# A Mamba mixer's input norm: where the second chunk's squares are taken, when its factors are requested, and how the third chunk's squares are added

## The chip, the cores and the metric

The program runs on one core of a Trainium2 chip. TensorE (PE) multiplies matrices, VectorE (DVE), ScalarE (ACT) and GpSimd (POOL) work on elements, and SyncE (SP) issues the transfers. Each engine works through its own list of instructions in order and waits on semaphores for the others. The metric is the device time of one execution in microseconds (us). TensorE's clock has two levels, 1.2 and 2.4 GHz; the profile gives the granted share of the higher one (0.50 or 1.00).

## The reference

One inference step of a two-layer decoder trunk: a Mamba-2 mixer with its MLP, then sliding-window attention with its MLP. The change is in the first operation of the mixer, the norm of its input, and touches the projection that follows:

```python
def rmsnorm(x, w):
    xf = x.astype(jnp.float32)
    xf = xf * lax.rsqrt(jnp.mean(xf * xf, axis=-1, keepdims=True) + EPS)
    return (xf * w.astype(jnp.float32)).astype(x.dtype)

def mamba_mixer(h, conv_state, ssm_state, norm_w, w_in, ...):
    zxbcdt = rmsnorm(h, norm_w) @ w_in
    ...
```

The model width is 1024. There are 1104 columns (tokens): 1024 of the prompt, 64 of the sample and 16 learned ones.

## The kernel before

Activations lie with the model width on the partitions: eight tiles of 128 rows (k = 0 to 7), and the 1104 columns in three chunks. The program's list of chunks (`CH`) holds (0, 384), (384, 384) and (768, 336); the mixer works on them in the order 2, 0, 1. This document calls them the first chunk (index 2, 336 columns), the second (index 0) and the third (index 1, 384 columns each). The lists of instructions of the engines are made by a scheduler that orders the whole program by its own estimate of times, so the order in the code is a wish and not a rule.

For each chunk the input norm goes through these steps:

1. `load_h` (L318) loads the input tiles `xt` in four pairs of k.
2. `sums_x` squares the eight tiles (L329, on ACT, into `xsq`), and sums over the partitions with a product of each square with a constant matrix `ones_r` (L333, on PE, plain fp32). With `add=True` the two squares of a pair are first added on DVE (L331), which halves the number of these sum products from eight to four. The buffers of `xsq` come from a ring of five (L237).
3. `rstd_x` makes the factors n = 1/sqrt(mean + eps) as exp(-0.5 ln(.)) on ACT: a Ln (L340) and an Exp (L342), each with a load of its function table ahead of it.
4. `norm_x` multiplies each tile by the norm's weight and the factors on DVE (L353), rounds it to the high part with a cast on ACT (L354), and takes the difference, the low part, into `S` (L356): on DVE for even k, on POOL for odd k.
5. `conv_mms` multiplies the chunk by the weights of two units, B and C: for each k three products per unit, high by high (L568), high weight by low part (L569), low weight by high part (L570); 48 products a chunk. The next steps copy the results out of PSUM on ACT (L579 to L583).

The weights of these two units are split in the same stretch: a cast on ACT (L170) and a difference of 128x1024 on POOL (L171) for each. After the third chunk's products follow those of the step sizes (L435, L436) and of the next units.

In the kernel before, the first chunk's squares are added in pairs; those of the second and third are not, and all are taken on ACT. The factors of the second and third chunk are asked for in one call, after the first chunk's products.

Of the kernel before, what the change touches and what calls it, by code (L numbers as in the profile page):

```python
# [10 lines left out]
AF = mybir.ActivationFunctionType  # L11
ALU = mybir.AluOpType
# [129 lines left out]
class Kernel:  # L142
# [175 lines left out]
            self.nc.sync.dma_start(out=hp[kp], in_=self.i["x"][:, 2 * kp:2 * kp + 2, o:o + n])  # L318
        return hp

    def sums_x(self, c, hp, tag, add=False):

        nc = self.nc
        n = CH[c][1]
        ms = self.psa.tile([P, 512], F32, tag=tag, bufs={"y": 2}.get(tag, 1), name="xms")
        for kp, h in enumerate(hp):
            sq = [self.n1("xsq")[:, :n] for _ in range(2)]
            for j in range(2):
                nc.scalar.activation(out=sq[j], in_=h[:, j], func=AF.Square)  # L329
            if add:  # L330
                nc.vector.tensor_tensor(out=sq[0], in0=sq[0], in1=sq[1], op=ALU.add)  # L331
            for j in range(1 if add else 2):
                nc.tensor.matmul(out=ms[:, :n], lhsT=self.ones_d, rhs=sq[j], start=(kp + j == 0),  # L333
                                 stop=(kp == 3 and (add or j == 1)))
        return ms[:, :n]
# [1569 lines left out]
    def mixer(self, c1):  # L1905

        nc = self.nc
        mp = self.pool("mixc", ctx=c1)
        self.sp = self.pool("sp", ctx=c1)
        self.psa = self.pool("psa", bufs=1, space=PSUM, ctx=c1)  # L1910
        xs, fm = {}, {}
        hp = {2: self.load_h(2)}
        us = [self.conv_unit(0, nm) for nm in ("B", "C")]
        hp[0] = self.load_h(0)
        hp[1] = self.load_h(1)
        self.mixer_consts(mp)
        ms2 = self.sums_x(2, hp[2], "cb", True)
        rs2 = self.rstd_x([ms2])[0]
        xs[2] = self.norm_x(2, hp[2], rs2)
        ms0 = self.sums_x(0, hp[0], "st")  # L1920
        ms1 = self.sums_x(1, hp[1], "y")
        self.conv_mms(us, 2, xs)
        rs0, rs1 = self.rstd_x([ms0, ms1])
        for c, rs in ((0, rs0), (1, rs1)):
            xs[c] = self.norm_x(c, hp[c], rs)
            self.conv_mms(us, c, xs)
        draw = self.dt_product(mp, xs)
        ux = self.conv_unit(0, "x0")
        fm["B"], fm["C"] = (self.conv_rest(u) for u in us)
        for c in CORD:  # L1930
            self.conv_mm(ux, c, xs)
        fm["x0"] = self.conv_rest(ux)
        sums = self.dt_path(mp, draw)
        next(sums)
        ux = self.conv_unit(0, "x1")
        for k, c in enumerate(CORD):
            if k == 1:
                next(sums, None)
            self.conv_mm(ux, c, xs)
        next(sums, None)  # L1940
        fm["x1"] = self.conv_rest(ux)
        for g in range(G):
            gate = None
            if g + 1 == G:
                y = [self.fm([P, T], "gy") for j in range(2)]
                space = lambda c: ((self.sp.tile([P, 1024], F32, tag="bm", bufs=1, name="gt") if c == 1 else
                                    self.cw.tile([P, T], F32, tag="th", bufs=1, name="gt"))[:, :768]
                                   .rearrange("p (j n) -> p j n", j=2))
                gate = self.gate_group(0, xs, y, space, lambda: self.fm([P, T], "gm"))
            for t in self.ssd(g, fm):  # L1950
                for k in range({8: 2, 2: 1, 3: 1, 6: 1, 7: 1}.get(t, 0) if gate is not None else 0):
                    next(gate)
            if g + 1 < G:
                fm = self.group_in(g + 1, xs)
        nc.sync.dma_start(out=self.o["conv"], in_=self.cvo)
        for _ in gate:
            pass
        return xs
# [68 lines left out]
```

## Time and profile before

| | |
|---|---|
| device time, median of 3 runs | 2925.34 us (2923.25 to 2930.92) |
| the profiled execution: its own time | 2923.57 us |
| the profiled execution: span of its instructions | 2921.9 us |
| busy in the span: PE, DVE, ACT, POOL | 96%, 65%, 48%, 47% |
| share of the chain that ended last: PE, DVE, ACT | 77%, 10%, 4% |
| the stretch that the change touches | 0 to about 56 us of the span |

The profiled execution lasts 1.67 us longer than its span, which is what lies around the instructions. It is 1.8 us shorter than the median. The busy shares are means over the whole program; the change lies in the first 2% of it, where PE still waits for the others.

### The profile page before, as it was taken

The numbers are of one execution on the slowest core, as the hardware profiler recorded it, in microseconds if no ns is written. First come the engines' busy times: TensorE is split into PE (matmuls) and PEld (weight loads), VectorE is DVE, ScalarE is ACT, GpSimd is POOL, SyncE is SP. The second block draws the span as 40 slices with busy tenths as digits, with TensorE's granted clock in tenths as the row PEclk, the third lists the DMA queues.
The fourth block names the chain that finished last, engine by engine and source line by source line (L and its number), as shares of the span: only waits on it lengthen the run. The fifth ranks groups of instructions, "written<-read, shape, count | busy, mean of one in ns | idle before, by whom it ended". The sixth has DMA issues, their size and how long they took to land.

```text
span 2921.9 us, 51729 instructions
## 1 busy us (share of the span) xinstructions
PE 2816.2 (96%) x19895; PEld 2711.0 (93%) x19895; DVE 1895.0 (65%) x2995; ACT 1413.9 (48%) x2742; POOL 1386.1 (47%) x1279
## 2 busy tenths in 40 slices
PE   8999999988989999999999999999999999999998
PEld 6999999978889999999999999988889999999998
DVE  6788777765657675455466765666678454356675
ACT  6555555544555264444343325655555444433333
POOL 5566666665546615444266573312112444345562
PEclk9999999999999999999999999999999999999998
DMA  3344544447655224444554422447453444533422
GB/s 137 91 128 124 125 128 123 123 123 258 218 206 171 80 85 149 136 156 139 224 212 171 161 89 94 160 153 261 164 187 133 150 140 150 206 138 124 151 96 73
DMA packets 219470, 433.43 MB, mean 148 GB/s; under 512 B 30728, under 2 KB 128392, under 8 KB 216648
## 3 DMA queue, kind: packets, MB, share of 16 engines
q1 hardware_dynamic: 219224, 430.14, 44.3%
q8 instruction: 156, 2.56, 0.4%
q14 instruction: 90, 0.74, 0.1%
HBM read 302.71 MB, written 128.32 MB: 148 GB/s over the span
## 4 chain that ended last, share of the span: by engine, by line
PE 77%; DVE 10%; ACT 4%; issue 3%; DMA 3%; POOL 3%; SPq 0%; DVEq 0%; ACTq 0%; POOLq 0%
PE g L204 10%; PE g L206 10%; PE g L205 10%; PE mc L204 4%; PE mc L206 3%; PE mc L205 3%; PE ma L204 3%; PE ma L205 3%; PE ma L206 3%; PE md L206 3%; PE md L205 3%; PE md L204 3%; PE mb L206 3%; PE mb L204 3%; PE mb L205 3%
## 5 line engine op out<-in xcount | busy, mean ns | idle before, releaser
L1048 POOL TENSOR_TENSOR w<-s,w 128x384 fp32r<-128x384 f32 (+1 forms) x272 | 370.4, 1368 | 386.9 <-ACT w L1047 354.4
L206 PE MATMUL g<-S,w 128*128 128x384 f32 (+2 forms) x1584 | 531.1, 336 | 3.9 <-POOL w L171 3.3
L204 PE MATMUL g<-S,w 128*128 128x384 f32 (+2 forms) x1584 | 533.4, 337 | 1.3 <-DVE qp L1462 0.6
L205 PE MATMUL g<-S,w 128*128 128x384 f32 (+2 forms) x1584 | 533.6, 337 | 0.0
L1048 POOL TENSOR_TENSOR w<-raw,w 128x384 fp32r<-128x384 f32 (+1 forms) x204 | 264.3, 1301 | 286.2 <-ACT w L1047 255.2
L171 POOL TENSOR_TENSOR w<-raw,w 128x1024 fp32r<-128x1024 f32 x96 | 247.1, 2574 | 253.3 <-ACT w L170 189.3
L206 PEld LDWEIGHTS g<-S,w 128*128 128x128 f32 x1584 | 301.9, 191 | 5.8 <-POOL w L171 3.6
L204 PEld LDWEIGHTS g<-S,w 128*128 128x128 f32 x1584 | 301.3, 190 | 4.7 <-issue 1.5
L205 PEld LDWEIGHTS g<-S,w 128*128 128x128 f32 x1584 | 301.7, 190 | 0.9 <-issue 0.3
L1047 ACT CAST w<-s 128x384 fp32r<-128x384 f32 (+1 forms) x272 | 149.8, 557 | 313.0 <-DVE s L1172 84.7
L204 PE MATMUL ma<-S,w 128*128 128x276 f32 (+1 forms) x808 | 235.2, 291 | 8.0 <-DVE us L1264 6.7
L206 PE MATMUL ma<-S,w 128*128 128x276 f32 (+1 forms) x808 | 234.7, 290 | 0.0
L205 PE MATMUL ma<-S,w 128*128 128x276 f32 (+1 forms) x808 | 234.3, 290 | 0.0
L1047 ACT CAST w<-raw 128x384 fp32r<-128x384 f32 (+1 forms) x204 | 111.8, 555 | 154.6 <-PE mc L206 45.2
L602 DVE SCALAR_TENSOR_TENSOR fm<-xp,cv,fm 128x1024 f32<-128x1024 f32 x96 | 162.8, 1698 | 33.1 <-ACT fm L583 32.5
L204 PEld LDWEIGHTS ma<-S,w 128*128 128x128 f32 x808 | 153.3, 190 | 9.3 <-ACT S L1229 2.7
L205 PE MATMUL g<-R,w 128*128 128x384 f32 (+2 forms) x480 | 158.6, 330 | 0.0
L204 PE MATMUL g<-R,w 128*128 128x384 f32 (+2 forms) x480 | 158.1, 329 | 0.0
L206 PE MATMUL g<-R,w 128*128 128x384 f32 (+2 forms) x480 | 158.1, 329 | 0.0
L205 PEld LDWEIGHTS ma<-S,w 128*128 128x128 f32 x808 | 153.5, 190 | 0.0
L206 PEld LDWEIGHTS ma<-S,w 128*128 128x128 f32 x808 | 153.2, 190 | 0.0
L170 ACT CAST w<-raw 128x1024 fp32r<-128x1024 f32 x96 | 100.5, 1047 | 105.8 <-DMA raw<-in_w_o_dram 19.9
(492 smaller groups left out, 8696.0 us busy)
## 6 DMA issues: line engine op xcount, KB each, us to landing
raw<-in_w_up_dram SPq DMA_DIRECT2D x64, 512.0 KB
raw<-in_w_in_dram SPq DMA_DIRECT2D x48, 512.0 KB
raw<-in_w_downs_dram SPq DMA_DIRECT2D x64, 384.0 KB
w<-ws_o SPq DMA_DIRECT2D x48, 512.0 KB
w<-ws_q SPq DMA_DIRECT2D x40, 512.0 KB
ab<-acs_d SPq DMA_DIRECT2D x64, 256.0 KB
S<-t_d SPq DMA_DIRECT2D x18, 828.0 KB
S<-t_e SPq DMA_DIRECT2D x18, 816.0 KB
```

The source lines that it names most:

```text
L170: nc.scalar.copy(out=wh, in_=raw)
L171: nc.gpsimd.tensor_tensor(out=wl, in0=raw, in1=wh.bitcast(F32), op=ALU.subtract)
L204: mm(out=out, lhsT=wh, rhs=xh, start=(first and k == 0), stop=False)
L205: mm(out=out, lhsT=wh, rhs=xl, start=False, stop=False)
L206: mm(out=out, lhsT=wl, rhs=xh, start=False, stop=(k == n - 1))
L602: nc.vector.scalar_tensor_tensor(out=acc[:, :SEQ], in0=xp[:, k:k + SEQ], scalar=cv[:, j, k:k + 1], in1=acc[:, :SEQ], op0=ALU.mult, op1=ALU ...
L1047: nc.scalar.copy(out=t[:, 0], in_=src)
L1048: nc.gpsimd.tensor_tensor(out=t[:, 1], in0=src, in1=t[:, 0].bitcast(F32), op=ALU.subtract)
```

## The change

`sums_x` gets a parameter `vector`: the squares of that many pairs are taken on DVE, as the product of a tile with itself, and the rest on ACT. The mixer calls it for the second chunk with `vector=3`, so six of the eight squares move to DVE. The third chunk's squares are now added in pairs. The factors of the second chunk are asked for right after the first chunk's norm and ahead of its products, those of the third after the second's norm, each in a call of its own.

```diff
-    def sums_x(self, c, hp, tag, add=False):
+    def sums_x(self, c, hp, tag, add=False, vector=0):
...
             for j in range(2):
-                nc.scalar.activation(out=sq[j], in_=h[:, j], func=AF.Square)
+                if kp < vector:
+                    nc.vector.tensor_tensor(out=sq[j], in0=h[:, j], in1=h[:, j], op=ALU.mult)
+                else:
+                    nc.scalar.activation(out=sq[j], in_=h[:, j], func=AF.Square)
...
-        rs2 = self.rstd_x([ms2])[0]
-        xs[2] = self.norm_x(2, hp[2], rs2)
-        ms0 = self.sums_x(0, hp[0], "st")
-        ms1 = self.sums_x(1, hp[1], "y")
-        self.conv_mms(us, 2, xs)
-        rs0, rs1 = self.rstd_x([ms0, ms1])
-        for c, rs in ((0, rs0), (1, rs1)):
-            xs[c] = self.norm_x(c, hp[c], rs)
+        rs = {2: self.rstd_x([ms2])[0]}
+
+        ms = self.sums_x(0, hp[0], "st", vector=3)
+        for c, nx in ((2, 0), (0, 1), (1, None)):
+            xs[c] = self.norm_x(c, hp[c], rs[c])
+            if nx is not None:
+                rs[nx] = self.rstd_x([ms])[0]
+            if nx == 0:
+                ms = self.sums_x(1, hp[1], "y", True)
             self.conv_mms(us, c, xs)
```

The line numbers of the changed kernel are four higher from the squares on (the ACT squares L329 become L333, the factors' Ln L340 becomes L344), and the new squares on DVE are L331.

The first place is DVE's list from the pair sums of the first chunk's squares to the first chunk's differences. `xsq` are squares, `xt` the input tiles, `n` the factors, `S` the low parts. Before:

```order
L331 TENSOR_TENSOR xsq<-xsq 128x336 x4
L426 MEMSET w 128x8x32
L353 SCALAR_TENSOR_TENSOR xt<-xt,nv,n_232 128x336 x8
L356 TENSOR_TENSOR S<-xt,S 128x336 x4
L456 TENSOR_SCALAR an<-an 128x32
```

And in the changed kernel:

```order
L335 TENSOR_TENSOR xsq<-xsq 128x336 x4
L331 TENSOR_TENSOR xsq<-xt 128x384 x2
L430 MEMSET w 128x8x32
L357 SCALAR_TENSOR_TENSOR xt<-xt,nv,n_232 128x336 x2
L331 TENSOR_TENSOR xsq<-xt 128x384 x2
L357 SCALAR_TENSOR_TENSOR xt<-xt,nv,n_232 128x336 x6
L331 TENSOR_TENSOR xsq<-xt 128x384 x2
L360 TENSOR_TENSOR S<-xt,S 128x336 x4
L335 TENSOR_TENSOR xsq<-xsq 128x384 x2
```

The six squares of the second chunk stand two ahead of the first chunk's scalings, two among them and two between them and the first chunk's differences.

The second place is ACT's list around the second chunk's factors, which are `n_365` before and `n_284` in the change. Before, from the last squares that stand ahead of them:

```order
L329 ACTIVATE xsq<-xt 128x384 x3
L411 ACTIVATE cv<-cv 128x32x5
L455 ACTIVATE an<-an 128x32
L427 CAST w<-raw 128x8x32
L429 CAST w<-raw 128x8x32
L329 ACTIVATE xsq<-xt 128x384
L340 ACT_TABLE_LOAD
L340 ACTIVATE n_365<-xms,eps 128x384
L329 ACTIVATE xsq<-xt 128x384
L342 ACT_TABLE_LOAD
L342 ACTIVATE n_365<-n_365 128x384
```

And in the changed kernel, where all these squares are of the third chunk:

```order
L333 ACTIVATE xsq<-xt 128x384 x3
L415 ACTIVATE cv<-cv 128x32x5
L333 ACTIVATE xsq<-xt 128x384
L459 ACTIVATE an<-an 128x32
L344 ACT_TABLE_LOAD
L344 ACTIVATE n_284<-xms,eps 128x384
L333 ACTIVATE xsq<-xt 128x384
L431 CAST w<-raw 128x8x32
L433 CAST w<-raw 128x8x32
L333 ACTIVATE xsq<-xt 128x384
L346 ACT_TABLE_LOAD
L346 ACTIVATE n_284<-n_284 128x384
```

The two casts of `w` and one more square now stand between the Ln and the Exp.

The third place is ACT's list around the third chunk's factors, `n_366` before and `n_392` in the change. Before, after the second chunk's casts:

```order
L354 CAST S<-xt 128x384 x7
L340 ACT_TABLE_LOAD
L340 ACTIVATE n_366<-xms,eps 128x384
L342 ACT_TABLE_LOAD
L342 ACTIVATE n_366<-n_366 128x384
L579 COPY xp<-g 128x256
```

And in the changed kernel:

```order
L358 CAST S<-xt 128x384 x8
L583 COPY xp<-g 128x256
L585 COPY xp<-g 128x10x8
L587 ACTIVATE fm<-g,cv 128x336
L583 COPY xp<-g 128x256
L585 COPY xp<-g 128x10x8
L587 ACTIVATE fm<-g,cv 128x336
L344 ACT_TABLE_LOAD
L344 ACTIVATE n_392<-xms,eps 128x384
L346 ACT_TABLE_LOAD
L346 ACTIVATE n_392<-n_392 128x384
```

The six copies of the first chunk's results (B and C, three each) now stand ahead of the third chunk's factors; before they stood behind.

## Rows read from the trace of the kernel before

**Rows 1.** Stretches 46.53 to 119 us: busy us (instructions) of each engine, granted clock, DMA
```profile
46.53:55.39 8.86, 8.86 (x48) 8.21 (x48) 3.86 (x7) 1.63 (x3) 2.37 (x3) 1.00 0.34 118
55.39:119.00 63.61, 63.61 (x408) 59.88 (x407) 48.03 (x61) 32.76 (x71) 28.80 (x32) 1.00 0.27 77
```

**Rows 2.** Waits of PE, 21 to 119 us: total, times, longest
```profile
PE g L569 <- DVE S L356: 1.7, 2, 1.1
PE g L569 <- DVE dx L477: 1.3, 1, 1.3
PE g L568 <- ACT fm L583: 0.6, 1, 0.6
```

**Rows 3.** Chain that ended last, 14 to 56 us: start, us, what
```profile
14.74 6.06 DVE xt L353 x8
...
21.28 0.42 PE g L569
...
23.39 0.66 PE xms L333 x2
24.07 0.52 ACT xsq L329
...
28.21 0.53 ACT n L342
28.77 6.62 DVE xt L353 x8
...
35.94 1.28 ACT L340
...
39.13 0.53 ACT n L342
...
46.53 0.45 PE g L569
```

**Rows 4.** Timeline of DVE, single instructions: start, us, what
```profile
14.74 0.77 DVE L353 SCALAR_TENSOR_TENSOR xt<-xt,nv,n 128x336 f32<-128x336 f32 x1 [5.01 <-ACT n L342]
16.40 0.55 DVE L353 SCALAR_TENSOR_TENSOR xt<-xt,nv,n 128x336 f32<-128x336 f32 x1
17.36 1.20 DVE L353 SCALAR_TENSOR_TENSOR xt<-xt,nv,n 128x336 f32<-128x336 f32 x1
```

**Rows 5.** Timeline of POOL, single instructions
```profile
10.49 2.35 POOL L171 TENSOR_TENSOR w<-raw,w 128x1024 fp32r<-128x1024 f32 x1 [5.16 <-ACT w L170]
12.81 2.34 POOL L171 TENSOR_TENSOR w<-raw,w 128x1024 fp32r<-128x1024 f32 x1
17.18 1.01 POOL L356 TENSOR_TENSOR S<-xt,S 128x336 fp32r<-128x336 f32 x1 [2.03 <-ACT S L354]
```

**Rows 6.** Timeline of SP's queue: an issue that waited for the second chunk's first pair
```profile
11.65 0.34 SPq L410 DMA_DIRECT2D cv<-in_cv_dram  x1
```

**Rows 7.** Timeline of PE's loads and products: two sums early, one late
```profile
13.36 0.34 PEld L333 LDWEIGHTS xms<-xsq,ones_r 128*128 128x128 f32 x1 [0.30 <-issue]
14.00 0.34 PEld L333 LDWEIGHTS xms<-xsq,ones_r 128*128 128x128 f32 x1 [0.30 <-issue]
...
29.86 0.81 PE L333 MATMUL xms<-xsq,ones_r 128*128 128x384 f32 x2
30.21 0.61 PE L570 MATMUL g<-S,w 128*128 128x336 f32 x1
```

**Rows 8.** Stretches around an idle time of PE at 2182 us, columns as in rows 1
```profile
2182.31:2185.75 3.44, 0.00 (x0) 0.03 (x1) 3.44 (x8) 0.00 (x0) 0.00 (x0) 1.00 1.06 396
2186.20:2189.60 3.40, 3.40 (x11) 2.99 (x10) 3.40 (x8) 0.00 (x0) 0.00 (x0) 0.50 1.05 415
```

**Rows 9.** Timeline of ACT: a weight cast, and the copies of the first chunk's results
```profile
22.84 0.39 ACT L427 CAST w<-raw 128x256 fp32r<-128x256 f32 x1
...
39.56 0.36 ACT L579 COPY xp<-g 128x256 f32<-128x256 f32 x1
...
41.35 0.54 ACT L354 CAST S<-xt 128x384 fp32r<-128x384 f32 x1
```

## Prediction

> **What bounds the kernel now.** I first read the stretches. From 55.39 to 119 us PE is busy for all of 63.61 us [rows 1], so whatever delays the end of the third chunk's products delays what follows, one for one. Ahead of that PE still waits for others. Between 21 and 119 us these waits are only 3.6 us [rows 2]: 1.3 for the second chunk's first difference (the row names a memset that stands beside it on DVE), 0.6 for a copy that frees a PSUM bank, 1.7 for two other differences, the longer one, 1.1, for the third chunk's. So after 21 us there is little to win. The chain of waits then shows what sets the start of each chunk's products [rows 3]: Exp (L342), eight scalings on DVE (L353), the first difference, the first low-part product (L569). The first chunk's low-part products begin at 21.28. The second chunk's Exp starts at 28.21 and its scalings at 28.77; they end at 35.39, the first difference 0.45 later, and PE goes on at about 35.9. The third chunk's Exp starts at 39.13 and ends at 39.66, and PE goes on at 46.53. Everything hangs on when each Exp is done and on what DVE then has to do until the first difference.
>
> One more thing comes from the timelines: DVE and POOL exclude each other when both work on two SBUF tensors. A scaling of 336 columns takes 0.55 us at 16.40 but 1.20 at 17.36, where POOL's difference runs from 17.18 to 18.19; it ends 0.37 us after POOL's. The scaling of 14.74 ends at 15.51, 0.36 us after POOL's weight difference of 12.81 to 15.15 [rows 4, 5]. So such a DVE instruction waits out POOL's and then needs about 0.4 us.
>
> The Trainium skill, "GPSIMD Engine Reference", Specifications, says that GpSimd's SBUF interfaces are shared with VectorE, with contention for DVE instructions in a two-port mode or with two SBUF inputs. The trace agrees (1.20 against 0.55 us). By that page the new squares, a tile times itself, should count as two inputs; without contention the sum would be that of the first rival below.
>
> **The change part by part.** *Four sums fewer on PE.* A sum costs 0.64 us early (13.36 to 14.00) and 0.35 late (29.86 to 30.21) [rows 7]. The four that go stood among the first chunk's products, at the late price: 1.4 us of PE's work. PE waits for the second chunk anyway, so this gives nothing unless that wait goes.
>
> *Squares on DVE.* The second chunk's first pair has landed at 11.65, when the SP issue that waited for it goes [rows 6]. POOL is then in the first weight difference, 10.49 to 12.84, with a second one of 2.34 us behind it [rows 5]. By the exclusion the first square ends at 13.2, the second weight difference then runs to 15.5, and the second square ends at 15.9. The first chunk's scalings, which waited for Exp until 14.74, now wait for these squares: behind a memset they start at about 16.05. No row shows a square on DVE; its bounds are nothing (a cost hidden ahead of Exp) and 1.2 us (a meeting with POOL). I take 0.5 where POOL is idle, from the scaling's 0.55, whose successor overlaps it a little. Two more squares stand after two scalings, and two after the other six. Stepping on with 0.5 for each, and three meetings with POOL's differences of odd k at 0.7 more each: two scalings to 17.1, two squares to 18.0, six scalings to 22.9, two squares to 23.8; the first difference meets POOL's last and ends at 24.85.
>
> *The second chunk's sums.* Now six of them stand on PE between the first high-part products and the first low-part one. The third and fourth are done by 18.9; the fifth waits for the fifth square, done at 23.4. The remaining four then cost the early price, 0.64 each, since PE has been nearly idle: done at 25.95. Before, this chunk's last sum was done at 24.05 [rows 3]. The first chunk's low-part products start at 25.95 instead of 21.28.
>
> *The second chunk's Exp.* Between the last sum and this Exp ACT had 4.2 us (24.05 to 28.21 [rows 3]), with one square ahead of Ln's table load and one behind Ln. What stands there now is more: the third chunk's second to fourth square must wait for buffers that the fifth to seventh sum free, so the fourth is done only at 25.9; behind it come a small scale (0.3), a square, a small Exp (0.2), and between Ln and Exp two weight casts and a further square. Against before that is one square of 0.5 [rows 3], two casts of 0.3 in steps (0.39 each [rows 9]) and the two small ones: 1.6 us more. With the sum 1.9 later Exp starts at 31.7 instead of 28.21. DVE waits behind it. Scalings and first difference took 7.1 us (28.77 to 35.84) and get a pair sum of 0.5 among them: done at 39.85, and PE goes on at 39.9 instead of 35.9, **+4.0**. PE has by then run out of the first chunk's products (at about 36), even if part of them runs at half the clock.
>
> *The third chunk's Exp.* It now stands behind the copies of the first chunk's results. ACT ends the second chunk's casts about when the first difference is done, 39.95 (before, 35.94), copies for 1.8 us (39.56 to 41.35 [rows 9]), and needs 3.7 us for two table loads, Ln and Exp (35.94 to 39.66 [rows 3]): done at 45.5, against 39.66. From there to the low-part product it was 6.9 us (to 46.53). In these POOL did nothing on two tensors during the scalings and met the differences; now the small work between them is gone (1.2 us, two tail products of the convolution), but the scalings meet POOL's differences, as the second chunk's do, up to three times 0.7. I take 6.9: 52.4 instead of 46.53. The copies now come early, so the wait of 0.6 inside the second chunk goes; PE ends that chunk at about 48.5 and idles for nearly 4 us. The third chunk's products take 8.86 us as before [rows 1]: done at 61.3 instead of 55.39, **+5.9 us**.
>
> *The clock.* An idle time of PE of 3.44 us (2182.31 to 2185.75) is followed by 3.40 us at a granted clock of 0.50, the lower of the two levels. In these 11 products start [rows 8]; at the rate of the third chunk's (48 in 8.86) it would be 18 [rows 1]. Seven products of 0.18 are **1.3 us**. The idle time ahead of the third chunk's products is of this size, so I add it once. A drop ahead of the second chunk's would only shorten the idle time ahead of the third.
>
> The Trainium skill, "TensorE: Matmul & The Clock Gate", Part 1, says that the lower clock is the default and that activity releases it. The trace agrees: sums cost 0.64 us early and 0.35 late. It speaks against this change, which makes PE's start sparser.
>
> No transfer is added or removed; SP's next load waits for a difference of this stretch and moves with it. The two places far behind where the scheduler orders anew (a norm sum a few products earlier, side products swapped) are on PE within one busy stretch: 0, and 1 us either way for the range.
>
> Sum: 5.9 + 1.3 = 7.2 us. On the profiled execution's own 2923.57 that is 2930.8; the median of the runs shown is 1.8 us higher and would give 2932.5. Between them I say **2931 us**, 0.2% slower.
>
> **The rivals.** *Squares that don't collide.* If POOL's weight differences let the squares pass, the first two are done by 12.7 and the scalings begin as before. Four squares still stand among them: first difference at 22.7, sums at 24.3, the second chunk's Exp 1.9 us later than before, the third's 4.2, and the end 4 us late at the full clock: 2927.6 on the own time. For it: the first scalings still fit. Against it: the scalings and differences that met POOL in this stretch all waited.
>
> *The faster side.* Place: the second chunk's first difference. If it is done before PE runs out of the first chunk's products, PE's waits go (3.6 us) and so does the work of four sums (1.4): at most 5.0 us, 2918.6 on the own time. It decides when that Exp starts 1.3 us earlier, at 26.9 or before. For it: ACT loses six squares. Against it: the fifth square alone, at 23.4, leaves four sums and 4 us of ACT's list in front. Even whole it is under 0.3%.
>
> *Slower by more.* If the third chunk's scalings meet POOL three times (2.1 us) with nothing regained, and the clock drops ahead of both later chunks and both drops count, it is 5.9 + 2.1 + 2.6, and 9 to 11 us in all: 2933 to 2935 on the own time. For it: from 13 to 23.4 us PE has only six sums and two products to do.
>
> **How the numbers follow.** Chances: my forecast (5 to 8.5 us slower) 0.45, no collision (0 to 5 slower) 0.24, the faster side 0.09, slower by more 0.22. What a measurement of this kernel can tell from no change is about 0.3%, 8.8 us; the three runs shown span 7.7. By that the fourth case, with a little of the first, is slower: 0.23. Of the faster side a third could be read as faster through the scatter: 0.03. The rest is the same: 0.74. The range takes in half of the faster side, 2 us below the median, and the fourth case's upper end with the median's offset: 2923 to 2938.
>
> **What would show it.** In the changed kernel's profile: two squares on DVE from about 11.7, each ending 0.4 us after a weight difference of POOL, the second near 15.9; the first chunk's scalings from 16; the second chunk's last sum at 26, its Exp near 32 and the third chunk's near 45; low-part products of the second chunk from 40 and of the third from 52, behind the latter's idle time a granted clock of 0.50; the step-size products (L439 there) from 61 or later. I am wrong if squares run through POOL's weight differences in 0.5 us, if ACT's waits for buffers are shorter than I stepped them, or if PE's clock rises sooner than its sparse work suggests.

## The result and the profile after

The changed kernel takes 2937.92 us in the median of five runs (2933.80 to 2939.62), the kernel before 2925.34 (2919.83 to 2930.92). The ratio is 1.0045, 95% interval 1.0032 to 1.0059: 12.6 us slower, where 5.7 were forecast (2931). The direction held and the range just held it (its upper end is 2938); the size did not. The profiled execution took 2937.92 us with a span of 2936.2 us, 14.3 more than before.

First the stretches that answer to [rows 1] and the clock's part of [rows 8]: the second chunk's late sums, the third chunk's products, and what follows them.

```profile
core 0: us, PE busy (x) PEld busy (x) DVE busy (x) ACT busy (x) POOL busy (x), PEclk, DMA share, GB/s
24.20:27.60 3.40, 3.40 (x8) 1.81 (x6) 2.56 (x5) 1.57 (x4) 1.67 (x4) 0.50 0.00 0
53.99:63.92 9.93, 9.93 (x47) 9.62 (x48) 2.18 (x3) 1.59 (x4) 0.82 (x1) 0.83 0.31 106
63.92:127.50 63.58, 63.58 (x408) 59.85 (x407) 48.01 (x61) 33.35 (x71) 28.38 (x32) 1.00 0.28 76
```

The last row is the one that carries the argument on: behind the third chunk's products PE is again busy throughout, 63.58 us against 63.61 before [rows 1]. So the delay of the step-size products, which start at 63.92 instead of 55.39, is handed on whole: **8.5 us of the loss arise in the first 64 us**. The third chunk's products start at 53.99 instead of 46.53 and take 9.93 us instead of 8.86, at a mean granted clock of 0.83.

The waits of PE between 27.5 and 127.5 us, to be read beside [rows 2]:

```profile
PE g L573 <- DVE S L360: 4.0, 2, 2.6
PE xms L337 <- DVE xsq L335: 1.6, 1, 1.6
```

Now DVE from 11.5 us (beside [rows 4]) and POOL (beside [rows 5]):

```profile
11.99 4.13 DVE L331 TENSOR_TENSOR xsq<-xt 128x384 f32<-128x384 f32 x2 [2.20 <-DMA xt<-in_x_dram]
16.12 0.27 DVE L430 MEMSET w<- 128x256 f32 x1
16.32 0.91 DVE L357 SCALAR_TENSOR_TENSOR xt<-xt,nv,n 128x336 f32<-128x336 f32 x2
17.15 1.01 DVE L331 TENSOR_TENSOR xsq<-xt 128x384 f32<-128x384 f32 x2
18.09 4.89 DVE L357 SCALAR_TENSOR_TENSOR xt<-xt,nv,n 128x336 f32<-128x336 f32 x6
22.90 1.01 DVE L331 TENSOR_TENSOR xsq<-xt 128x384 f32<-128x384 f32 x2
23.84 1.62 DVE L360 TENSOR_TENSOR S<-xt,S 128x336 fp32r<-128x336 f32 x2
```

```profile
10.74 4.96 POOL L171 TENSOR_TENSOR w<-raw,w 128x1024 fp32r<-128x1024 f32 x2 [5.41 <-ACT w L170]
17.80 1.13 POOL L360 TENSOR_TENSOR S<-xt,S 128x336 fp32r<-128x336 f32 x1 [2.10 <-ACT S L358]
```

Two squares take 4.13 us beside POOL's two weight differences, and 1.01 us where POOL is idle when each of them starts (at 17.15 and 22.90). They end 0.4 us behind POOL (16.12 against 15.70), as forecast; the first chunk's scalings start at 16.32 instead of 14.74 [rows 4]. The last two squares start only at 22.90.

PE's sums behind them, and then the factors on ACT:

```profile
18.18 2.75 PE L337 MATMUL xms<-xsq,ones_r 128*128 128x384 f32 x4
23.50 4.54 PE L337 MATMUL xms<-xsq,ones_r 128*128 128x384 f32 x8 [2.57 <-DVE xsq L331]
27.55 0.64 PE L573 MATMUL g<-S,w 128*128 128x336 f32 x1
```

```profile
29.69 0.58 ACT L344 ACTIVATE n<-xms,eps 128x384 f32<-128x384 f32 x1
30.17 0.51 ACT L333 ACTIVATE xsq<-xt 128x384 f32<-128x384 f32 x1
30.58 0.39 ACT L431 CAST w<-raw 128x256 fp32r<-128x256 f32 x1
30.88 0.40 ACT L433 CAST w<-raw 128x256 fp32r<-128x256 f32 x1
31.18 0.52 ACT L333 ACTIVATE xsq<-xt 128x384 f32<-128x384 f32 x1
31.72 1.28 ACT L346 ACT_TABLE_LOAD   x1
33.02 0.53 ACT L346 ACTIVATE n<-n 128x384 f32<-128x384 f32 x1
...
42.37 0.67 ACT L587 ACTIVATE fm<-g,cv 128x336 f32<-128x336 f32 x1
43.06 1.28 ACT L344 ACT_TABLE_LOAD   x1
...
46.24 0.53 ACT L346 ACTIVATE n<-n 128x384 f32<-128x384 f32 x1
```

Four sums are eight instructions here: a sum of plain fp32 is two instructions on PE, and the eight run from 23.50, and from 24.2 on at a granted clock of 0.50, as the first stretch above shows. The first low-part product starts at 27.55 (before 21.28 [rows 3]). The second chunk's Exp starts at 33.02 (before 28.21), with two squares and two casts between Ln and the Exp's table load; the third chunk's at 46.24 (before 39.13), behind the first chunk's copies and both its table loads. So the second Exp is 4.8 us late and the third 7.1: 13.22 us lie between the two, where it was 10.92 before, and the six copies now stand between them (41.09 to 43.04).

That is 8.5 of 14.3 us of span. The rest arises later. Behind 2178 us the trace names three waits of PE. The first stands against 3.4 us before (2182.31 to 2185.75 [rows 8]), the second against 3.2 us, the third against nothing:

```profile
PE g L204 <- DMA w<-ws_o: 4.8, 1, 4.8
PE md L204 <- ACT w L1051: 3.1, 1, 3.1
PE mc L204 <- DVE rx L1081: 1.5, 1, 1.5
```

### The profile page after: what moved, and what is told of

Its sections match the earlier page's. It is cut to its first block, busy times and chain, and to the rows that moved or that the text cites. A ratio compares the mean times of both kernels' runs of the same rounds, so it can differ in the third digit from the quotient of the medians.

```text
span 2936.2 us, 51715 instructions
## 1 busy us (share of the span) xinstructions
PE 2816.6 (96%) x19887; PEld 2711.5 (92%) x19887; DVE 1901.2 (65%) x3005; ACT 1413.3 (48%) x2736; POOL 1380.1 (47%) x1279
## 4 chain that ended last, share of the span: by engine, by line
PE 55%; DVE 5%; issue 4%; DMA 3%; POOL 1%; ACT 1%; SPq 0%; DVEq 0%; POOLq 0%; ACTq 0%
PE g L204 5%; PE g L206 5%; PE g L205 5%; PE mc L204 3%; PE mc L206 3%; PE mc L205 3%; PE ma L204 3%; PE ma L206 3%; PE ma L205 3%; PE md L205 3%; PE md L206 2%; PE md L204 2%; PE mb L206 2%; PE mb L205 2%; PE mb L204 2%
## 5 line engine op out<-in xcount | busy, mean ns | idle before, releaser
L204 PEld LDWEIGHTS ma<-S,w 128*128 128x128 f32 x808 | 153.0, 189 | 12.0 <-ACT w L1051 4.8
L205 PEld LDWEIGHTS ma<-S,w 128*128 128x128 f32 x808 | 153.1, 190 | 0.0
L204 PE MATMUL mc<-S,w 128*128 128x276 f32 (+1 forms) x512 | 148.6, 290 | 4.6 <-DVE hh L1268 3.1
```

The costliest lines, as they stand in the source:

```text
L204: mm(out=out, lhsT=wh, rhs=xh, start=(first and k == 0), stop=False)
L205: mm(out=out, lhsT=wh, rhs=xl, start=False, stop=False)
```

## The experiments

Two questions were open: which part of the change costs the 8.5 us at the front, and whether the other 4 us come from the places far behind, where the scheduler orders anew although the code there is untouched. In what follows "lag" is the start of the step-size products (L439) less 55.4, and "new order" is an order behind 640 us other than that of before. In the lists of PE, DVE, ACT and SP that difference is there for every kernel which adds the third chunk's squares in pairs or squares on DVE, and not for the early request alone. It has three forms: that of the change, that of the squares on DVE alone, and one that all the others share.

**The change without its squares on VectorE.**

```diff
-        ms = self.sums_x(0, hp[0], "st", vector=3)
+        ms = self.sums_x(0, hp[0], "st")
```

> The change without its squares on VectorE: all of the second chunk's squares stay on ScalarE; the factors' order and the third chunk's pair adds are those of the change. In the change's trace the step-size products start 8.5 us later than before (63.9 against 55.4). Theory: the squares on VectorE cause this, through six late sums at 1.28 us each; here the second chunk's Exp starts within 1.5 us of before's 28.2, and the step-size products within 2.5 us of 55.4. Rival 1, the third chunk's Exp behind the copies of the first chunk's results: the second Exp is on time, the third is still late (43 or later), and the step-size products start 4 us or more late. The places far behind are ordered anew here too: if these cost, as the second rival has it, the whole is slower than the lag at the step-size products by 3 to 5 us; if that remainder of the change was scatter, the two agree within 2 us.

Measured: 2930.42 us, ratio 1.0022 (1.0013 to 1.0031). The second Exp starts at 29.69, the third at 40.63, the step-size products at 57.4: a lag of 2.0 where the change has 8.5. The squares on DVE are worth 6.5 of it, with all that moves along with them. One thing that moves is the copies, which rival 1 is about:

```profile
37.40 0.58 ACT L344 ACTIVATE n<-xms,eps 128x384 f32<-128x384 f32 x1
38.28 0.37 ACT L583 COPY xp<-g 128x256 f32<-128x256 f32 x1
...
40.63 0.52 ACT L346 ACTIVATE n<-n 128x384 f32<-128x384 f32 x1
41.06 0.35 ACT L583 COPY xp<-g 128x256 f32<-128x256 f32 x1
```

Here the third chunk's Ln is ahead of all six copies, and only one unit's three stand ahead of its Exp; the distance from the second Exp to the third is 10.94 us, as before (10.92). So the copies cost nothing here, and rival 1 as the cause of the whole lag falls, since the second Exp of the change is late already. But in the change all six stand ahead of Ln, and the distance is 13.22: there they are worth 2.3 of the 8.5 us, close to the 1.8 that the prediction gave them. The whole is 6.3 us slower than before, 4.3 more than the lag.

**Only the squares on VectorE.** The code of before, with this call:

```diff
-        ms0 = self.sums_x(0, hp[0], "st")
+        ms0 = self.sums_x(0, hp[0], "st", vector=3)
```

> The kernel before with one part of the change: the second chunk's six squares on VectorE; both later factors are asked for behind the first chunk's products as before, the third chunk's squares are summed one by one. Theory: the squares on VectorE are the cost, so the step-size products start 6 to 10 us later than before (61 to 65), since eight more sums of the third chunk stand on TensorE as well. Rival 1, the third chunk's Exp behind the copies: here that Exp stands ahead of the copies again, so the step-size products start at most 4 us late. Far places are ordered anew, in a form of their own.

Measured: 2930.81 us, 1.0025 (1.0015 to 1.0034). The step-size products start at 60.3, a lag of 4.9: less than the 6 I set as the least, so without the other two parts the squares cost somewhat less. The Exps start at 34.01 and 44.92.

**Only the pair adds.** The code of before, with this call:

```diff
-        ms1 = self.sums_x(1, hp[1], "y")
+        ms1 = self.sums_x(1, hp[1], "y", True)
```

> The kernel before with one part of the change: the third chunk's squares added in pairs on VectorE, so four sums fewer on TensorE. Theory: worth little here, because the second chunk's Exp sets the pace: the step-size products start between 2 us earlier and 1 us later than before's 55.4 (four sums of two instructions are 2.6 us at the later price). Rival 1: without the sums of the third chunk its Ln and Exp move, and if the copies go ahead of them, as in the change, the products start 3 us or more late. Far places: this kernel has the same new order there as the first of these four with hardly a lag ahead of it; if that order costs, the whole is 3 to 5 us slower than the step-size products' lag says, otherwise within 2 us of it.

Measured: 2930.10 us, 1.0020 (1.0012 to 1.0029); step-size products at 58.1. Four sums fewer on PE, and a lag of 2.7 us, outside what the theory gave (1 at most). ACT's timeline shows where: from 24.5 us on three of the third chunk's squares, a small scale and the two weight casts stand ahead of the table load of the second chunk's Ln, which starts at 26.86 (before, one square at 24.07 [rows 3] and then the load); its Exp starts at 30.46 instead of 28.21. One unit's copies do stand between the third chunk's Ln and Exp, but that Exp (41.40) is late by no more than the second. Some of the lag lies ahead of all this: the first chunk's scalings start at 15.60 instead of 14.74.

**Only the early request.** The change's loop, with all squares on ACT and none added in pairs:

```diff
-        ms = self.sums_x(0, hp[0], "st", vector=3)
+        ms = self.sums_x(0, hp[0], "st")
...
-                ms = self.sums_x(1, hp[1], "y", True)
+                ms = self.sums_x(1, hp[1], "y")
```

> The change's order of requests alone: each chunk's factors are asked for ahead of the products of the chunk before, all squares on ScalarE, none of the third chunk's added in pairs. Only a handful of instructions change places, all within the first 60 us: a square of the third chunk stands behind the second chunk's Exp instead of ahead of its Ln, a sum moves by one product. All theories: the step-size products within 1.5 us of before's 55.4, the whole within 3 us of before. If it is slower by more than that, the early request itself costs, and the theory that the squares on VectorE do is in doubt. Nothing is ordered anew far behind, so its later lag is a measure of scatter between two profiled executions.

Measured: 2920.10 us, 0.9989 (0.9981 to 0.9998); step-size products at 54.5, nothing ordered anew far behind. It is the one part that does no harm, and 0.1% faster than the kernel before. It was run again:

> The change's order of requests alone, once more on another chip, because its first measurement (0.9989, 0.9981 to 0.9998) ends close to no change. If asking early is worth 2 to 4 us by itself, the ratio is again 0.9986 to 0.9995 with an interval below 1; if the first result was scatter, the interval takes in 1.

Measured: 2922.92 us, 0.9991 (0.9982 to 1.0000); step-size products at 54.4. The two agree, though the second interval touches 1, so by itself it does not rule out scatter. Taken together this is a version that is 1.5 to 4 us faster than the kernel before in its medians, about 1 of which is seen at the step-size products.

**One pair and two pairs on VectorE.** The change with `vector=1` and `vector=2` instead of 3:

> The change with only the first of the second chunk's three pairs squared on VectorE (two squares, the ones that meet POOL's weight differences); the far order is within two rows that of the change without VectorE squares (2930.4 us, step-size products at 57.4). Theory, the late sums cost: the first pair's sums are early anyway, so the step-size products start within 1.5 us of 57.4 and the whole is within 2 us of 2930.4. Rival, the meeting with POOL is the cost, since it holds the first chunk's scalings until 16.3: 3 us or more over both already here.

> The change with two of the three pairs on VectorE: two squares ahead of the first chunk's scalings, two behind the second scaling; the far order is that of the change without VectorE squares, row for row (2930.4 us, 57.4). Theory, the late sums cost: the pair that the change squares last, behind all eight scalings, is on ScalarE here; the second chunk's Exp starts at 30 to 31.5 instead of 33.0, the step-size products at 57 to 60, the whole at 2930 to 2933. Rival, the meeting with POOL: about as late as the whole change (62 to 64; 2935 to 2937).

Measured: one pair 2930.64 us, 1.0023 (1.0014 to 1.0032), step-size products at 58.3; two pairs 2932.28 us, 1.0024 (1.0015 to 1.0033), products at 59.8. With none, one, two and three pairs the lag is 2.0, 2.9, 4.4 and 8.5. The first pair meets POOL for as long as in the change and adds 0.9; the third, squared last, behind all eight scalings, adds 4.1. So the meeting with POOL is the small part, as the theory had it, and what the third pair brings the large one. Of that the late sums show at the second Exp, which starts at 29.69, 30.68, 30.92 and 33.02 in the four kernels. The copies add to it: with two pairs and with three all six stand ahead of the third chunk's Ln, and the two Exps are 12.39 and 13.22 us apart, with none or one 10.9. With two pairs the second chunk's Exp starts at 30.92, in the range given:

```profile
29.49 1.28 ACT L459 ACT_TABLE_LOAD   x1
30.78 0.23 ACT L459 ACTIVATE an<-an 128x32 f32<-128x32 f32 x1
30.92 0.51 ACT L346 ACTIVATE n<-n 128x384 f32<-128x384 f32 x1
```

**An instruction of one input in place of the square.** It leaves out the squares of the second chunk:

```diff
-                    nc.vector.tensor_tensor(out=sq[j], in0=h[:, j], in1=h[:, j], op=ALU.mult)
+                    nc.vector.tensor_scalar(out=sq[j], in0=h[:, j], scalar1=0.0, scalar2=1.0, op0=ALU.mult, op1=ALU.add)
```

> The change with its six VectorE squares replaced by an instruction of one input (times zero plus one), so that the second chunk's factors are wrong: it leaves out the squares. The question is only whether such an instruction waits for POOL's weight difference. Theory, two inputs from SBUF and POOL exclude each other: the first one, started while POOL's difference runs, takes about 0.3 to 0.6 us, and the first chunk's scalings start by 14.5 instead of 16.3. Rival, any VectorE instruction on SBUF waits: 1.5 and 2.7 us as in the changed kernel (13.50 and 16.11 as ends).

The timeline of DVE, as above:

```profile
11.97 3.73 DVE L331 TENSOR_SCALAR xsq<-xt 128x384 f32<-128x384 f32 x2 [2.24 <-DMA xt<-in_x_dram]
15.70 0.27 DVE L430 MEMSET w<- 128x256 f32 x1
15.90 0.91 DVE L357 SCALAR_TENSOR_TENSOR xt<-xt,nv,n 128x336 f32<-128x336 f32 x2
16.73 0.61 DVE L331 TENSOR_SCALAR xsq<-xt 128x384 f32<-128x384 f32 x2
```

The pair takes 3.73 us beside POOL and 0.61 alone: it waits like the square, and the scalings start at 15.90, not by 14.5. The theory that two inputs are what makes it wait falls, and the rival holds for this instruction. The whole took 2937.70 us in one run.

**The far order, taken away and put in.** One product of the state recurrence is repeated into the same bank near 640 us, so that the scheduler's estimate sees TensorE a little later. With six in the change, the lists behind them are those of before. With eleven in the kernel before, they were expected to be those of the change, but are not: by the trace they have the form that the change without VectorE squares has. So that run tells what a new order costs, and not what the change's order does. With four in the kernel before, nothing moves beyond a few instructions near 640 us.

```diff
-            nc.tensor.matmul(out=cb[:n, :n], lhsT=Bf[:, c0:c0 + n], rhs=Cf[:, c0:c0 + n], start=True, stop=True)
+            nc.tensor.matmul(out=cb[:n, :n], lhsT=Bf[:, c0:c0 + n], rhs=Cf[:, c0:c0 + n], start=True, stop=True); [nc.tensor.matmul(out=cb[:n, :n], lhsT=Bf[:, c0:c0 + n], rhs=Cf[:, c0:c0 + n], start=True, stop=True) for _ in range(6) if (g, t) == (7, 6)]
```

(eleven, and four, at `(7, 5)` in the two others.)

> The changed kernel with six more products: a product of the state recurrence (the last group's seventh block of tokens, near 640 us) is done seven times instead of once, into the same bank, which leaves the result as it is. Its only purpose is that the scheduler, whose model sees TensorE a little later, then puts every instruction behind that point in the order of the kernel before; up to there the order is that of the change. The step-size products' lag should be the change's, 8 to 9 us. Theory that the far order costs 3 to 5 us: behind the six products the lag stays where it is, and the whole is 8 to 9 us slower than before plus the price of the six products (two instructions of 0.28 each per product, at most 3.3 us, read from the lag on both sides of them). Rival, that it is scatter or comes from the shift itself: the lag grows again by 3 to 5 us behind 2180 us, and the whole is 12 to 13 us slower plus the six products.

> The kernel before with eleven more products of the same kind (the last group's sixth block of tokens), behind which the scheduler's order is that of the changed kernel in every place from there on; ahead of them it is that of before. Lag at the step-size products: 0. Theory that the far order costs: behind the eleven products (at most 6 us) 3 to 5 us more are lost, about 1 near 880 us and the rest between 2180 and 2265 us. Rival, scatter or shift: nothing more is lost, within 1.5 us.

> The kernel before with four such products more, at a place where the scheduler changes nothing else: the price of the extra products alone. Between 0 and 2.2 us slower than before, by the same for all theories; the two kernels beside it are read against it.

Two anchors of PE for each, the step-size products and the last stage of attention (first and last start are behind the durations). The last stage of attention before:

```profile
L1522 PE MATMUL yb<-mb,vm x128: 270/275/377, 1836.7 to 2172.7; 128*128 128x128 f32 x128
```

The change:

```profile
L439 PE MATMUL g<-S,w x24: 311/334/343, 63.9 to 71.6; 128*64 128x384 f32 x16, 128*64 128x336 f32 x8
L1526 PE MATMUL yb<-mb,vm x128: 270/275/378, 1847.3 to 2181.9; 128*128 128x128 f32 x128
```

The change with the far order of before:

```profile
L439 PE MATMUL g<-S,w x24: 311/334/343, 62.5 to 70.1; 128*64 128x384 f32 x16, 128*64 128x336 f32 x8
L1526 PE MATMUL yb<-mb,vm x128: 270/275/377, 1843.8 to 2180.0; 128*128 128x128 f32 x128
```

The kernel before with a new far order:

```profile
L439 PE MATMUL g<-S,w x24: 310/334/343, 55.1 to 62.8; 128*64 128x384 f32 x16, 128*64 128x336 f32 x8
L1526 PE MATMUL yb<-mb,vm x128: 270/274/377, 1843.2 to 2177.4; 128*128 128x128 f32 x128
```

Measured: the change with the old far order 2932.30 us, 1.0035 (1.0022 to 1.0047), 9.0 us slower than the kernel before beside it; the kernel before with the new far order 2931.70 us, 1.0028 (1.0018 to 1.0039), 8.4 us slower; with four products alone 2922.47 us, 0.9997 (0.9988 to 1.0006). So the extra products cost nothing that can be measured four at a time, and at most 0.55 us each (two instructions of 0.275). Of the eleven nothing is seen either: the lag of that kernel is -0.3 at the step-size products and -0.7 at the last product of the state recurrence (664.3 against 665.0), behind them.

The first number is the main one: with the change's own first 640 us, a lag of 7.1 and six products more, the kernel takes 9.0 us more than before, where the change takes 12.6. The intervals of the two (1.0035 and 1.0045) overlap, so the medians alone do not part them; the traces do. Without the new order the lag stays: 7.1 at the step-size products, 7.3 at the last stage of attention (2180.0 against 2172.7 before), 7.6 at the span's end (2929.5 against 2921.9). In the change the last stage is 9.2 late and the end 14.3. From the last product of attention to the span's end it is 749.2 us before, 749.5 in the change with the old order and 750.5 to 751.3 in the three others with the old order; in the change it is 754.3 and in its variant with one input 754.0. The other new orders lie between: four at 752.5 to 753.0, the squares alone at 750.1 and the kernel before with the new order at 751.1, which the old order reaches too.

The kernel before with the new order has no lag at the start (-0.3). Its attention's last stage starts 6.5 late, ends 4.7 late, and the end is 6.6 late. So most of its loss arises between 665 and 1837 us, where its lists differ from those of before only between 880 and 910. In the same stretch the early request run again, with the lists of before, went from -2.1 to +0.5. Its 8.4 us are clear of scatter (interval 1.0018 to 1.0039), but no place of its trace can be named for them.

All medians less the lag, side by side (us; the two with six and eleven products contain them):

| kernel | far order | median against before | lag | rest |
|---|---|---|---|---|
| the change | new | +12.6 | 8.5 | 4.1 |
| without VectorE squares | new | +6.3 | 2.0 | 4.3 |
| one pair on VectorE | new | +6.2 | 2.9 | 3.3 |
| two pairs on VectorE | new | +7.8 | 4.4 | 3.4 |
| only squares on VectorE | new | +6.7 | 4.9 | 1.8 |
| only pair adds | new | +6.0 | 2.7 | 3.3 |
| before with a new order | new | +8.4 | -0.3 | 8.7 |
| early request | old | -4.0 | -0.9 | -3.1 |
| early request again | old | -1.5 | -1.0 | -0.5 |
| before with four products | old | -0.9 | 1.7 | -2.6 |
| the change with the old order | old | +9.0 | 7.1 | 1.9 |

A lag is read from one execution, and the kernel before itself, with four products added far behind, shows 1.7, and the change's own first 640 us show 8.5 and 7.1 in two kernels; so a single rest can be off by that much. Taken together the seven with a new order lie between 1.8 and 8.7 and the four with the old between -3.1 and 1.9.

What differs behind 2178 us is, first, the wait for a load of weights near 2182 us. PE's waits of the kernel before with the new order, behind 2178 us:

```profile
PE g L204 <- DMA w<-ws_o: 3.6, 1, 3.6
PE md L204 <- ACT w L1051: 2.7, 1, 2.7
PE ma L204 <- ACT n L1097: 1.2, 1, 1.2
```

And of the change with the old order:

```profile
PE g L204 <- DMA w<-ws_o: 3.4, 1, 3.4
PE md L204 <- ACT w L1051: 3.2, 1, 3.2
```

The first wait is 3.4 to 3.8 us in the five traces with the old order, 4.7 to 4.9 in six with a new one, and 3.6 and 3.8 in the two other new ones. A wait of 1.5 and 1.8 us for `rx` behind 2265 us stands only in the two traces with the change's own order, and there DVE takes two 128x512 instructions on `s` (L1061, 3.12 us from 2270.44) ahead of the `rx` (L1081, at 2273.48), where before the `rx` came first (L1077, at 2258.59) and they followed at 2259.22: this wait follows from the order. The first wait is longer by as much as SP's queue takes longer for the load's two issues. In the change, and before:

```profile
2184.44 3.64 SPq L163 DMA_DIRECT2D w<-ws_o  x2
```

```profile
2175.45 2.22 SPq L163 DMA_DIRECT2D w<-ws_o  x2
```

They take 1.4 us longer. What holds them up was not settled. The far order alone does not settle it: between 910 and 2190 us the lists are the same in all kernels, and the kernel before with the new order has these issues in 2.81 us, where four others with its far order take 3.48 to 3.59. The two waits together are about 3 us of the change's rest; the remainder is spread in pieces that single executions do not tell apart from scatter.

## Why the prediction was too small

**The bound.** Right: PE is busy throughout behind the third chunk's products, and their delay is handed on.

**Squares on DVE.** Right in place and size: ends at 16.1 (15.9 forecast), scalings at 16.3 (16.05), last pair of squares at 22.9 to 23.9 (23.8), first difference from 23.84. The Trainium skill, "GPSIMD Engine Reference", Specifications, gives a shared SBUF interface and contention for VectorE instructions in a two-port mode or with two SBUF inputs. The square agrees: 4.13 us for two against 1.01. The instruction of one input waited as well, 3.73 against 0.61, so two inputs are not needed; that agrees with the page only if it runs in a two-port mode, which no run here shows directly.

**The second chunk's sums.** The step was right and the term mis-sized. I took 0.64 us as the price of a sum, from the distance of two starts [rows 7], but those were the two instructions of one sum (and so is the 0.35 half a sum, which enters no sum of the forecast). Four late sums cost 4.05 us (23.50 to 27.55) instead of 2.6, and the first low-part product came at 27.55, not 25.95. The Trainium skill, "TensorE: Matmul & The Clock Gate", Part 1, says that the lower clock is the default and activity releases it. The trace agrees: PE has nothing to do from 20.9 to 23.5 us; the sums start then, and from 24.2 us on they run at a granted clock of 0.50.

**The second and third Exp.** From there each step came out late by that amount: second Exp at 33.0 (31.7 forecast), third Exp done at 46.8 (45.5). From there to the first low-part product it took 7.2 us, where I had taken 6.9 and put the full meetings with POOL into a rival. So the third chunk's products start at 54.0 (52.4). The copies ahead of the third Exp, which were forecast, held.

**The clock.** In the change's profile right: 1.07 us (9.93 against 8.86), forecast 1.3, at the place named. But it is no fixed price of the change. In the change with the old order, whose lists are the same up to there, PE waited only 1.6 us instead of 2.6 ahead of the third chunk's products; they started at 53.86 and took 8.6 us at a granted clock of 1.00.

All of the front together: 8.5 us in the change's profile, 7.1 in the kernel that shares its first 640 us, 7.2 forecast. The late sums are in both (27.55 and 27.13 against 25.95), so the 1.4 between the two is the clock. In the change's profile the late sums are the 1.3 above the forecast; in the other one they and the missing drop of the clock cancel, and that 7.1 agrees with 7.2 is luck.

**The base.** The sum was 7.2 us, but the 2931 stands only 5.7 above the median of before, because it was set between the profiled execution's own time and the median. That choice took 1.5 us off. With it, the 6.9 us by which the change is above the forecast are 1.5 from the base, 1.3 from the front and 4.1 from the far places.

**The far places.** Here the prediction failed. I put them at "0, and 1 us either way" because they lie within a busy stretch of PE. That is so for PE's own list, which changes from 880 to 895 and from 2196 to 2206 us, where PE was busy 14.87 of 15 and all of 10 us. But the lists of DVE and ACT change on to 2266, and from 2206 to 2270 PE was busy only 60.48 of 64 us. What the runs show in place of the 0: from the last product of attention to the end the change takes 5.1 us more than before (754.3 against 749.2), and 749.5 with the old order restored; and the six other kernels with a new order are 1.8 to 8.7 us slower than their lags say. Of the 5.1 the wait for `rx` (1.5) follows from the order; why the load at 2182 is issued more slowly (1.4) and where the rest arises stays open.

**The rivals.** "Squares that don't collide" was wrong about the premise, though the meeting turned out to be the small part (0.9 us for the first pair). "The faster side" needed a second Exp by 26.9; only the early request comes near (28.1, a lag of -0.9). "Slower by more" came nearest in its number, and its meeting of the third chunk with POOL happened, but its reasons do not cover the far part.

## What to carry to other kernels

Where a scheduler orders the whole program by estimated times, compare the whole lists of instructions and not the edited stretch: here about a third of the loss arose more than 600 us behind the edit. A harmless extra instruction ahead of such a place is a way to measure it, once the lists of the kernel that it makes have been compared too. Moving work off an engine helps only if the consumer gets it earlier; squares on VectorE arrived behind eight scalings, and the sums behind them ran on a TensorE that had fallen to half its clock. Of three parts made together, measure each alone: one gave 0.1%, and the two others took far more.

## What the hardware showed that was not expected

A VectorE instruction with a single SBUF input (times zero plus one, fp32) waits out a GpSimd instruction as a two-input one does: 3.73 us for two beside 128x1024 differences, 0.61 alone. A sum of plain fp32 over 384 columns is two TensorE instructions. Two issues of one weight load on SyncE's queue took 3.64 us in the change and 2.22 before, between the same neighbours in the queue. And the granted clock of the third chunk's products was 0.83 in one execution and 1.00 in another behind the same lists of instructions.
